# Hybrid attention layer on one core: float32 products of the head tasks moved behind the rounded ones, and some head steps moved later

## The chip, the cores and the metric

The kernel runs on one core of a Trainium2 chip. A core has TensorE (PE, matrix products; its weight loads are listed apart as PEld), VectorE (DVE), ScalarE (ACT), GpSimd (POOL) and SyncE (SP, which only issues transfers). The metric is the device time of one execution in microseconds; three runs of the kernel before took 1094.37, 1094.30 and 1093.46 us, so its median is 1094.3 us.

## What is computed

One layer of a streaming encoder, 256 tokens of width 2048, all float32, cut here to what matters:

```python
h  = rms_norm(x, attn_norm)
qa, ka, va, fa, qb, kb, vb = split(h @ w_in)          # 8 + 8 heads of width 128
# forgetting heads: q and k normed per head, c = cumsum(log_sigmoid(fa + b))
logits = q @ k.T * scale + c[t] - c[s]                # causal
out_a  = softmax(logits) @ va
# stick-breaking heads
z = qb @ kb.T * scale                                 # strictly causal
suffix = reverse_cumsum(log_sigmoid(z) - z) - itself
out_b  = exp(log_sigmoid(z) + suffix) @ vb
x = x + concat(rms_norm(out_a), rms_norm(out_b)) @ w_out
x = x + conv_ffn(rms_norm(x))                         # up, conv of 3, SiLU gate, down
```

## The kernel before

Every weight matrix is streamed in pieces of 1 MB and multiplied in three rounded products: a piece is split into a high part (w_hi, a cast on ScalarE, L263) and a low part (w_lo, a subtraction on VectorE, L271), the tokens likewise, and high x high, high x low and low x high are summed in PSUM. A *step* is one such piece. In the stage of the heads a step's products are twelve of 512 columns (L291; eight with w_hi, four with w_lo), or twice that. The order on every engine is the order in which the Python code issues the instructions. In each round of the main loop, the weights of the step two ahead are split, those six ahead are loaded, the step's products are issued, and then `tick()` is called; steps of 24 products call it a second time in their middle.

`tick()` is what weaves the heads between the weight products. Each head is a Python generator; `running` holds those under way, and a tick advances each of them to its next `yield`. A new head starts at the earliest three ticks after the last. So a head's instructions of one `yield` stretch stand on each engine between the products of two steps, and the next stretch follows one tick later.

A forgetting head (`fox_head`) goes through these stretches. First it splits its queries and keys into rounded parts (qk, L725 and L726). Two ticks later come the scores in PSUM tile ps_s: a rounded product of 384 columns with the forget sums (L731), the first 128 x 128 block in full float32 (L734, which TensorE runs as two passes), and three rounded products of 256 columns for the second block (L736); then VectorE adds the mask and takes the maxima (L739 to L742). Two ticks later ScalarE takes exponentials and VectorE normalises (L748 to L753). Two ticks later TensorE transposes the three blocks of weights into ps_p (L758, float32). One tick later they are split (pT, L763 to L765). One tick later, two where the head's number divides by four, they are multiplied with the values into ps_o: three rounded products (`weighted`, L709) and a float32 one (L710). One tick later the output is scaled and squared for the norm.

A stick-breaking head (`sb_head`) multiplies its queries and keys in float32 right at its start (ps_z, L785 and L786), and masks them on VectorE (L789). One tick later ScalarE runs three activations and VectorE one operation (e, L792 to L795). Two ticks later that is split (sps, L799 and L800). Two ticks later the running sums are added in ps_z by rounded products: for the high part one of 384 columns (L805) and one of 128 (L806), then the same for the low part. One tick later come the exponential and its split (w and ws, L809 to L813), one tick later `weighted` (the last head has float32 products only, L821), and one tick later the output.

Other float32 products of the stage are the transposes of queries and keys when a group of four heads is ready (ps_h, L637) and a few small sums (pg, L927). Head tiles in PSUM share four banks. At the end of the stage the heads still running are advanced inside the output projection, whose last products need their results.

Of the kernel before, what the change touches and what calls it, by code (L numbers as in the profile page):

```python
# [15 lines left out]
P = 128  # L16
D = 2048
S = 256
# [3 lines left out]
NH = 8  # L22
# [16 lines left out]
LOAD, SUM, SPLIT = 6, 4, 2  # L39
WARM = 4, 2  # L40
STAGGER = 3
FFN_PARTS = [(f, min(f + 8, NFT)) for f in range(0, NFT, 8)]


@with_exitstack
def hybrid_layer(
# [19 lines left out]
    nc = tc.nc  # L66
# [153 lines left out]
    steps, following, after, waiting, running, others = [], [], [], deque(), [], []  # L220
# [8 lines left out]
    def advance(tasks):  # L229
        tasks[:] = [g for g in tasks if next(g, g) is not g]  # L230

    def tick():
        ticks[0] += 1
        if waiting and ticks[0] - ticks[1] >= STAGGER:
            running.append(waiting.popleft())
            ticks[1] = ticks[0]
        advance(running)
        advance(others)

    def acc_tile(name):  # L240
# [88 lines left out]
    ntri = masksR[:, 2 * P :]  # L329
# [341 lines left out]
    def sb_rows(half):  # L671
        def done(rows):
            while started["fox"] < NH or started["sb"] < 4 * half:
                yield
            if half:
                yield
                yield
            yield from to_heads(rows, (f"qB{half}", f"kB{half}"), (QSCALE, 1.0))
            ready.add(f"qB{half}")
            if "vB" in ready:  # L680
                start_sb(half)

        return done
# [22 lines left out]
    def weighted(po, hi, lo, v1, w, w1):  # L706
        mm = nc.tensor.matmul
        for m, (v, i) in enumerate(((hi, 0), (hi, 1), (lo, 0))):
            mm(po, v, w[:, i, :S], start=m == 0, stop=False)  # L709
        mm(po[:, P:], v1, w1, start=False, stop=True)  # L710

    def squared(po, group, h):
# [7 lines left out]
    def fox_head(h, half):  # L720
        q, k = tile_of[f"qA{half}"][:, h % 4, :], tile_of[f"kA{half}"][:, h % 4, :]
        hi, lo, v1 = tile_of["vA"]
        qk = tmp.tile([P, 2, 3 * P], F32R, name="qk", tag="sps")
        for c, whole in ((slice(0, P), q[:, P:]), (slice(P, 3 * P), k)):
            act.copy(qk[:, 0, c], whole)  # L725
            dve.tensor_tensor(qk[:, 1, c], whole, f32(qk[:, 0, c]), op=ALU.subtract)  # L726
        yield
        yield
        ps = psb.tile([P, 512], F32, name="ps_s", tag="t")[:, : 3 * P].rearrange("p (a b) -> p a b", a=3)
        s0, s1 = ps[:, 0, :], ps[:, 1:3, :].rearrange("p a b -> p (a b)")  # L730
        nc.tensor.matmul(  # L731
            ps.rearrange("p a b -> p (a b)"), headR[:, h : h + 1].to_broadcast([P, P]), cR, start=True, stop=False
        )
        nc.tensor.matmul(s0, q[:, :P], k[:, :P], start=False, stop=False)  # L734
        for a, b in ((0, 0), (0, 1), (1, 0)):
            nc.tensor.matmul(s1, qk[:, a, :P], qk[:, b, P:], start=False, stop=a == 1)  # L736
        started["fox"] += 1
        diagonal = ps[:, 0::2, :]
        dve.tensor_tensor(diagonal, diagonal, maskF, op=ALU.add)  # L739
        nm = small.tile([P, NT], F32, name="nm", tag="nm", bufs=4)  # L740
        dve.tensor_reduce(nm[:, 0:1], s0, axis=AX.X, op=ALU.max, negate=True)
        dve.tensor_reduce(nm[:, 1:2], s1, axis=AX.X, op=ALU.max, negate=True)  # L742
        yield
        yield
        l = small.tile([P, NT], F32, name="l", tag="l", bufs=4)
        pr = tmp.tile([P, 3, P], F32, name="pr", tag="pr")
        p0, p1 = pr[:, 0, :], pr[:, 1:3, :].rearrange("p a b -> p (a b)")
        act.activation(p0, s0, AF.Exp, bias=nm[:, 0:1], accum_out=l[:, 0:1])  # L748
        act.activation(p1, s1, AF.Exp, bias=nm[:, 1:2], accum_out=l[:, 1:2])
        rl = small.tile([P, NT], F32, name="rl", tag="rl", bufs=4)  # L750
        dve.reciprocal(rl, l)
        dve.tensor_scalar(p0, p0, rl[:, 0:1], None, op0=ALU.mult)
        dve.tensor_scalar(p1, p1, rl[:, 1:2], None, op0=ALU.mult)  # L753
        yield
        yield
        pt = psb.tile([P, 512], F32, name="ps_p", tag="t")[:, : 3 * P].rearrange("p (a b) -> p a b", a=3)
        for i in range(3):
            nc.tensor.transpose(pt[:, i, :], pr[:, i, :], ident)  # L758
        yield
        pT = tmp.tile([P, 2, 3 * P], F32R, name="pT", tag="sps")  # L760
        p1 = tmp.tile([P, 3 * P], F32, name="p1", tag="pT")[:, :P]
        flat = pt.rearrange("p a b -> p (a b)")
        act.copy(pT[:, 0, :S], flat[:, :S])  # L763
        act.copy(p1, flat[:, S:])
        dve.tensor_tensor(pT[:, 1, :S], flat[:, :S], f32(pT[:, 0, :S]), op=ALU.subtract)  # L765
        yield
        if h % 4 == 0:
            yield
        po = psb.tile([P, S], F32, name="ps_o", tag="t")
        hs = slice(h * HD, (h + 1) * HD)  # L770
        weighted(po, hi[:, hs], lo[:, hs], v1[:, hs], pT, p1)
        yield
        act.activation(oFox[:, h, :], po, AF.Identity, scale=g_fox[:, h : h + 1])
        sq = squared(po, 0, h)
        if sq is not None:
            dve.tensor_tensor(ssq[0], ssq[0], sq, op=ALU.add)

    def sb_head(h, half):
        q, k = tile_of[f"qB{half}"][:, h % 4, :], tile_of[f"kB{half}"][:, h % 4, :]
        (hi, lo), v1 = tile_of["vB01"], tile_of["vB"][half, 1]  # L780
        ps = psb.tile([P, 512], F32, name="ps_z", tag="t")[:, : 3 * P].rearrange("p (a b) -> p a b", a=3)
        z0, z1 = ps[:, 0:2, :].rearrange("p a b -> p (a b)"), ps[:, 2, :]
        zz = ps.rearrange("p a b -> p (a b)")
        mm = nc.tensor.matmul
# [9 lines left out]
        act.activation(e, e, AF.Ln, bias=1.0)  # L794
        dve.scalar_tensor_tensor(e, zz, 0.0, e, op0=ALU.max, op1=ALU.add)  # L795
        yield
        yield
        sps = tmp.tile([P, 2, 3 * P], F32R, name="sps", tag="sps")
        act.copy(sps[:, 0, :], e)  # L799
        dve.tensor_tensor(sps[:, 1, :], e, f32(sps[:, 0, :]), op=ALU.subtract)  # L800
        yield
        yield
        for i in range(2):
            s = sps[:, i, :]
            mm(zz, ntri[:, :P], s, start=False, stop=False, skip_group_check=True)  # L805
            mm(ps[:, 1, :], ntri[:, P:], s[:, 2 * P :], start=False, stop=i == 1, skip_group_check=True)  # L806
        yield
        w = tmp.tile([P, 3 * P], F32, name="w", tag="pT")
        act.activation(w, zz, AF.Exp)  # L809
        if h < NH - 1:  # L810
            ws = tmp.tile([P, 2, 3 * P], F32R, name="ws", tag="sps")
# [3 lines left out]
        po = psb.tile([P, S], F32, name="ps_o", tag="t")  # L815
        hs = slice((h % 4) * HD, (h % 4 + 1) * HD)
        h0 = slice(h * HD, (h + 1) * HD)
        if h < NH - 1:
            weighted(po, hi[:, h0], lo[:, h0], v1[:, hs], ws, w[:, S:])
        else:  # L820
            mm(po, tile_of["vB"][half, 0][:, hs], w[:, :S], start=True, stop=False)  # L821
            mm(po[:, P:], v1[:, hs], w[:, S:], start=False, stop=True)
        yield
# [465 lines left out]
    for f_lo, f_hi in FFN_PARTS:  # L1289
# [5 lines left out]
        if last is None:  # L1295
            behind = []
# [5 lines left out]
        behind = deque(behind)  # L1302
# [116 lines left out]
```

## Time and profile before

| what | value |
|---|---|
| runs of the kernel before, median | 1094.3 us |
| profiled execution, span from the first to the last instruction | 1091.8 us |
| TensorE busy in it | 1087.3 us, 5701 products |
| VectorE busy | 924.2 us |
| ScalarE busy | 755.1 us |
| read from memory | 255.48 MB, 236 GB/s over the span |

The profile is of one execution. It gives no total of its own for that execution beside the span; the median lies 2.5 us above the span, which is what is outside the first and last instruction. In timelines a row gives the start and the length in us from the span's start, the engine, the line of the kernel, what is written from what, the shape and how many alike follow each other. Matmuls are pipelined, so that the records overlap: what a product takes from its engine is read from one start to the next, not from its length. A number in square brackets is idle time ahead of a row and who ended it. A list of waits gives the sum, the times and the longest. A row of windows gives, for each engine, busy time and instructions, then the granted clock of TensorE, the share of the DMA engines and GB/s.

### The profile page before, as it was taken

The page shows a single profiled execution, that of the slowest core. Times are in us where ns is not written, and L with a number is a line of the kernel's source. Part 1 is how long each engine was busy: PE and PEld are TensorE (multiplying, and loading weights), DVE is VectorE, ACT ScalarE, POOL GpSimd, SP SyncE. Part 2 cuts the span into 40 slices and gives each one's busy share as a digit, 9 for nine tenths or more (in the row PEclk, how much of TensorE's full clock was granted, in tenths as well). Part 3 has the DMA queues.
Part 4 walks back from the last instruction along what each step waited for, and adds up shares of the span by engine and source line. Part 5 has one row for each costly group of instructions (what it writes and reads, how often), then busy time and mean ns, then how long its engine had stood idle before and what let it go on. Part 6 is the DMA issues. An engine that isn't in the chain of part 4 may idle for free.

```text
span 1091.8 us, 14685 instructions
## 1 busy us (share of the span) xinstructions
PE 1087.3 (100%) x5701; PEld 939.5 (86%) x5701; DVE 924.2 (85%) x918; ACT 755.1 (69%) x968; POOL 59.0 (5%) x53
## 2 busy tenths in 40 slices
PE   9999999999999999999999999999999999999998
PEld 9988888888888888888888888888888888888887
DVE  5988899888897667779887988889898889879996
ACT  6767697767766657767766776677667767667763
POOL 0000000001000000000000000100000000000000
PEclk9999999999999999999999999999999999999999
DMA  8897886868777465669989597996969799896995
GB/s 310 276 272 239 271 206 196 253 183 271 239 214 251 154 199 161 214 170 249 288 206 316 173 265 254 254 296 170 302 195 271 241 246 279 215 319 161 291 247 155
DMA packets 175215, 258.53 MB, mean 237 GB/s; under 512 B 4632, under 2 KB 98218, under 8 KB 175146
## 3 DMA queue, kind: packets, MB, share of 16 engines
q1 hardware_dynamic: 151690, 210.26, 56.9%
q0 software_dynamic: 23280, 47.19, 24.5%
q8 instruction: 45, 0.74, 0.3%
q14 instruction: 24, 0.20, 0.1%
q10 hardware_dynamic: 176, 0.14, 0.0%
HBM read 255.48 MB, written 2.10 MB: 236 GB/s over the span
## 4 chain that ended last, share of the span: by engine, by line
PE 100%; DVE 0%; issue 0%
PE pu L1153 45%; PE bank_a L291 18%; PE bank_b L291 11%; PE bank_c L291 6%; PE acc_o L291 6%; PE acc_v L411 4%; PE bank_e L291 2%; PE acc L291 2%; PE ps_x L192 1%; PE ps_h L637 1%; PE ps_o L709 1%; PE ps_z L785 0%; PE ps_o L710 0%; PE ps_z L805 0%; PE ps_i L186 0%; PE half L291 0%
## 5 line engine op out<-in xcount | busy, mean ns | idle before, releaser
L271 DVE TENSOR_TENSOR w_lo<-w_raw,w_hi 128x2048 fp32r<-128x2048 f32 (+2 forms) x251 | 555.9, 2219 | 124.1 <-ACT w_hi L263 123.1
L263 ACT CAST w_hi<-w_raw 128x2048 fp32r<-128x2048 f32 (+2 forms) x251 | 464.6, 1854 | 220.7 <-PE pu L1153 90.0
L1153 PE MATMUL pu<-hT,w_hi 128*128 128x512 f32 x1408 | 333.6, 390 | 0.0
L1153 PEld LDWEIGHTS pu<-hT,w_hi 128*128 128x128 f32 x1408 | 263.1, 188 | 53.6
L1153 PEld LDWEIGHTS pu<-hT,w_lo 128*128 128x128 f32 x1408 | 180.0, 191 | 6.5
L1153 PE MATMUL pu<-hT,w_lo 128*128 128x256 f32 x1408 | 182.1, 283 | 0.0
L1206 POOL DMA_DIRECT2D w_raw<-in_w_down_dram x31 | 39.8, 1302 | 715.9 <-DVE w_lo L271 384.7
L1078 ACT ACTIVATE tap<-up,ccol 128x256 f32<-128x256 f32 x176 | 74.6, 495 | 0.0
L291 PE MATMUL bank_a<-w_hi,hT 128*128 128x512 f32 x192 | 48.5, 395 | 0.0
L291 PEld LDWEIGHTS bank_a<-w_hi,hT 128*128 128x128 f32 x192 | 35.2, 188 | 6.7
L291 PE MATMUL bank_b<-w_hi,s 128*128 128x512 f32 x160 | 40.1, 393 | 0.0
L291 PE MATMUL bank_a<-w_hi,s 128*128 128x512 f32 x160 | 40.0, 392 | 0.0
L291 PE MATMUL bank_a<-w_hi,g 128*128 128x512 f32 x152 | 38.0, 392 | 0.0
L411 PE MATMUL acc_v<-w_hi,hT 128*128 128x344 f32 x192 | 35.7, 328 | 0.0
L291 PEld LDWEIGHTS bank_b<-w_hi,s 128*128 128x128 f32 x160 | 28.8, 189 | 5.5 <-issue 0.3
L291 PEld LDWEIGHTS bank_a<-w_hi,s 128*128 128x128 f32 x160 | 28.9, 189 | 5.2
L1083 DVE TENSOR_TENSOR gate<-gate,tap 128x512 f32<-128x512 f32 x44 | 30.3, 689 | 2.7 <-DVE gate L1083 0.5
L1083 DVE TENSOR_TENSOR val<-val,tap 128x512 f32<-128x512 f32 x44 | 30.3, 689 | 2.3
L291 PE MATMUL acc_o<-w_hi,oSb 128*128 128x512 f32 x128 | 31.8, 397 | 0.0
L1064 DVE TENSOR_TENSOR up<-t,R 128x512 f32<-128x512 f32 x44 | 30.5, 692 | 1.5
L291 PEld LDWEIGHTS bank_a<-w_hi,g 128*128 128x128 f32 x152 | 27.4, 189 | 4.9
L411 PEld LDWEIGHTS acc_v<-w_hi,hT 128*128 128x128 f32 x192 | 30.4, 190 | 0.5 <-DVE hT L203 0.2
(293 smaller groups left out, 1411.2 us busy)
## 6 DMA issues: line engine op xcount, KB each, us to landing
w_raw<-in_w_up_dram SPq DMA_DIRECT2D x88, 1024.0 KB, 7.0
w_raw<-in_w_down_dram SPq DMA_DIRECT2D x44, 1024.0 KB, 6.7
w_raw<-in_w_in_dram SPq DMA_DIRECT2D x40, 1024.0 KB, 5.5
w_raw<-in_w_down_dram POOLq DMA_DIRECT2D x31, 1024.0 KB, 9.8
w_raw<-in_w_out_dram SPq DMA_DIRECT2D x16, 1024.0 KB, 7.7
w_raw<-in_w_in_dram POOLq DMA_DIRECT2D x10, 1024.0 KB, 9.4
w_raw<-in_w_in_dram SPq DMA_DIRECT2D x13, 516.0 KB, 5.5
xb<-in_x_dram POOLq DMA_DIRECT2D x4, 512.0 KB, 8.7
```

Of the source, the lines that this page charges most:

```text
L192: nc.tensor.transpose(ps[:, j, t * P : (t + 1) * P], x2[:, t, (k + j) * P : (k + j + 1) * P], ident)
L263: copy(hi[:, :n], raw[:, :n])
L271: dve.tensor_tensor(lo[:, :n], raw[:, :n], f32(hi[:, :n]), op=ALU.subtract)
L291: nc.tensor.matmul(o, lhs(i, l, t), r[:, i, :] if cut is None else r[:, i, cut], start=starts and j == 0, stop=stops and j == 3 * n - 1, s ...
L411: nc.tensor.matmul(banks[j][t][:, :VC], of_half(hT[:, k], l, t), w[:, 0, m * VC : (m + 1) * VC], start=k == l == 0 and w is mem["parts", i ...
L637: nc.tensor.transpose(ps[:, h, :], rows[n, t][:, h * HD : (h + 1) * HD], ident)
L709: mm(po, v, w[:, i, :S], start=m == 0, stop=False)
L1064: dve.tensor_tensor(u[:, :, 2:], t2, R, op=ALU.mult)
L1078: act.activation(taps[w][:, j, :], u[:, j, w : w + S], AF.Copy, scale=ccol[:, w, f : f + 1])
L1083: dve.tensor_tensor(a, a, tap, op=ALU.add)
L1153: nc.tensor.matmul(acc[:, j, S:] if low else acc[:, j, :], (lo if low else hi)[:, i, j * P : (j + 1) * P], hT[:, k, 0, :] if low else hT[: ...
L1206: nc.gpsimd.dma_start(mem[weights].rearrange("p (a b) -> p a b", a=4), plus, accum_op=ALU.add)
```

## The change

The order in which a tick advances the heads is made of two passes. A head may now stop with `yield FLOATS`. In the first pass every head is advanced by one `yield`; those that stopped with `FLOATS` are then advanced once more, in a second pass of the same tick. So the rounded products of all heads in a tick stand ahead of their float32 ones. `FLOATS` stands ahead of the float32 scores, the transposes, the float32 product of `weighted` and the first scores of stick-breaking.

Some steps also move in time. In forgetting heads 0 to 6 the transposes come four ticks after the exponentials instead of two, and the weighting two ticks after the split of the transposed weights, instead of one (two for heads 0 and 4). Head 7 keeps its distances. A stick-breaking head makes its first scores one tick after its start instead of at once; its split (sps) follows the activations after one tick instead of two, so that the later parts keep their distance from the start of the head. The queries and keys of the second group of stick-breaking heads are transposed one tick earlier. The sums are ordered as two products of 384 columns and then two of 128. The number and the shapes of the instructions are the same.

```diff
+    def advance_heads():
+        kept, behind = [], []
+        for g in running:
+            said = next(g, g)
+            if said is not g:
+                kept.append(g)
+            if said == FLOATS:
+                behind.append(g)
+        advance(behind)
+        running[:] = kept
...
-        advance(running)
+        advance_heads()
         advance(others)
...
             if half:
                 yield
-                yield
             yield from to_heads(rows, (f"qB{half}", f"kB{half}"), (QSCALE, 1.0))
...
             mm(po, v, w[:, i, :S], start=m == 0, stop=False)
+        yield FLOATS
         mm(po[:, P:], v1, w1, start=False, stop=True)
...
-        nc.tensor.matmul(s0, q[:, :P], k[:, :P], start=False, stop=False)
         for a, b in ((0, 0), (0, 1), (1, 0)):
-            nc.tensor.matmul(s1, qk[:, a, :P], qk[:, b, P:], start=False, stop=a == 1)
+            nc.tensor.matmul(s1, qk[:, a, :P], qk[:, b, P:], start=False, stop=False)
+        yield FLOATS
+        nc.tensor.matmul(s0, q[:, :P], k[:, :P], start=False, stop=True)
...
-        yield
-        yield
+        aligned = h < NH - 1
+        for _ in range(4 if aligned else 2):
+            yield
+        yield FLOATS
         pt = psb.tile([P, 512], F32, name="ps_p", tag="t")[:, : 3 * P].rearrange("p (a b) -> p a b", a=3)
...
-        if h % 4 == 0:
+        if aligned:
             yield
...
         (hi, lo), v1 = tile_of["vB01"], tile_of["vB"][half, 1]
+        yield
+        yield FLOATS
         ps = psb.tile([P, 512], F32, name="ps_z", tag="t")[:, : 3 * P].rearrange("p (a b) -> p a b", a=3)
...
         dve.scalar_tensor_tensor(e, zz, 0.0, e, op0=ALU.max, op1=ALU.add)
         yield
-        yield
         sps = tmp.tile([P, 2, 3 * P], F32R, name="sps", tag="sps")
...
         for i in range(2):
-            s = sps[:, i, :]
-            mm(zz, ntri[:, :P], s, start=False, stop=False, skip_group_check=True)
-            mm(ps[:, 1, :], ntri[:, P:], s[:, 2 * P :], start=False, stop=i == 1, skip_group_check=True)
+            mm(zz, ntri[:, :P], sps[:, i, :], start=False, stop=False, skip_group_check=True)
+        for i in range(2):
+            mm(ps[:, 1, :], ntri[:, P:], sps[:, i, 2 * P :], start=False, stop=i == 1, skip_group_check=True)
```

What stands in a row on TensorE around the fourth forgetting head's scores, before (ps_o is a weighting, p and pT its float32 and rounded operands, ps_s scores, ps_p transposes of weights, ps_h transposes of queries and keys, bank_ weight products):

```order
L709 MATMUL ps_o<-pT,vA_712 128x256 x2
L709 MATMUL ps_o<-pT,vA_713 128x256
L710 MATMUL ps_o<-p_1554,vA_714 128x128
L731 MATMUL ps_s<-cR,headR 128x384
L734 MATMUL ps_s<-kA_1190,qA_1222 128x128
L736 MATMUL ps_s<-qk 128x256 x3
L291 MATMUL bank_b<-w_hi,hT 128x512 x8
L291 MATMUL bank_b<-w_lo,hT 128x512 x4
L758 MATMUL ps_p<-cs,pr 128x128 x3
L637 MATMUL ps_h<-cs,rB_1045 128x128 x4
L637 MATMUL ps_h<-cs,rB_1046 128x128 x4
```

The same place after the change:

```order
L720 MATMUL ps_o<-pT,vA_712 128x256 x2
L720 MATMUL ps_o<-pT,vA_713 128x256
L743 MATMUL ps_s<-cR,headR 128x384
L747 MATMUL ps_s<-qk 128x256 x3
L722 MATMUL ps_o<-p_1515,vA_714 128x128
L773 MATMUL ps_p<-cs,pr 128x128 x3
L749 MATMUL ps_s<-kA_1190,qA_1222 128x128
L303 MATMUL bank_b<-w_hi,hT 128x512 x8
L303 MATMUL bank_b<-w_lo,hT 128x512 x4
L649 MATMUL ps_h<-cs,rB_1045 128x128 x4
L649 MATMUL ps_h<-cs,rB_1046 128x128 x4
```

Three float32 runs (L710, L734, and L758 with L637) have become two: the float32 products of weighting, transposes and scores stand in one run behind all rounded ones. The weighting is now that of the first head, where it was that of the second.

TensorE around the third stick-breaking head's first scores (ps_z; the weighting is that of the first head), before:

```order
L785 MATMUL ps_z<-qB_2093,kB_2060 128x256
L786 MATMUL ps_z<-qB_2093,kB_2060 128x128
L291 MATMUL bank_b<-w_hi,sums 128x512 x8
L291 MATMUL bank_b<-w_lo,sums 128x512 x4
L709 MATMUL ps_o<-ws,vB_2285 128x256 x2
L709 MATMUL ps_o<-ws,vB_2286 128x256
L710 MATMUL ps_o<-w,vB_1874 128x128
L291 MATMUL bank_c<-w_hi,hT 128x512 x8
```

And after:

```order
L303 MATMUL bank_b<-w_hi,sums 128x512 x8
L303 MATMUL bank_b<-w_lo,sums 128x512 x4
L720 MATMUL ps_o<-ws,vB_2285 128x256 x2
L720 MATMUL ps_o<-ws,vB_2286 128x256
L722 MATMUL ps_o<-w,vB_1870 128x128
L802 MATMUL ps_z<-qB_2080,kB_2046 128x256
L803 MATMUL ps_z<-qB_2080,kB_2046 128x128
L303 MATMUL bank_c<-w_hi,hT 128x512 x8
```

The first scores stand one step later, behind the float32 product of the weighting, so two runs have become one.

VectorE around the fifth and sixth stick-breaking heads (ws: the low parts that the fifth head's weighting needs; xb: rows of the output projection; sps: the split of the sixth head), before:

```order
L795 SCALAR_TENSOR_TENSOR e<-ps_z,e 128x384
L900 SCALAR_TENSOR_TENSOR xb<-bank_a,nrg_127,xb 128x512
L271 TENSOR_TENSOR w_lo<-w_raw,w_hi 128x2048
L900 SCALAR_TENSOR_TENSOR xb<-bank_b,rg_125,xb 128x512
L271 TENSOR_TENSOR w_lo<-w_raw,w_hi 128x2048
L813 TENSOR_TENSOR ws<-w,ws 128x256
L800 TENSOR_TENSOR sps<-e,sps 128x384
L789 TENSOR_TENSOR ps_z<-ps_z,masksR 128x2x128
```

And after:

```order
L812 SCALAR_TENSOR_TENSOR e<-ps_z,e 128x384
L917 SCALAR_TENSOR_TENSOR xb<-bank_a,nrg_127,xb 128x512
L283 TENSOR_TENSOR w_lo<-w_raw,w_hi 128x2048
L829 TENSOR_TENSOR ws<-w,ws 128x256
L816 TENSOR_TENSOR sps<-e,sps 128x384
L917 SCALAR_TENSOR_TENSOR xb<-bank_b,rg_125,xb 128x512
L283 TENSOR_TENSOR w_lo<-w_raw,w_hi 128x2048
L806 TENSOR_TENSOR ps_z<-ps_z,masksR 128x2x128
```

ws and sps stand ahead of one row update and one subtraction of weights, where they stood behind them. On TensorE the fifth head's weighting has moved ahead by half a step as well, from the middle of the next step's products to the end of the step before.

More of the change, by code (lines that the diff above doesn't have):

```diff
@@ L41 @@
 STAGGER = 3
+FLOATS = "float32 products"
 FFN_PARTS = [(f, min(f + 8, NFT)) for f in range(0, NFT, 8)]
@@ L770, in fox_head @@
         hs = slice(h * HD, (h + 1) * HD)
-        weighted(po, hi[:, hs], lo[:, hs], v1[:, hs], pT, p1)
+        yield from weighted(po, hi[:, hs], lo[:, hs], v1[:, hs], pT, p1)
         yield
@@ L818, in sb_head @@
         if h < NH - 1:
-            weighted(po, hi[:, h0], lo[:, h0], v1[:, hs], ws, w[:, S:])
+            yield from weighted(po, hi[:, h0], lo[:, h0], v1[:, hs], ws, w[:, S:])
         else:
+            yield FLOATS
             mm(po, tile_of["vB"][half, 0][:, hs], w[:, :S], start=True, stop=False)
```

## The prediction

> **What bounds the kernel now.** I read the page first, then the stage of the heads alone (busy time by windows), then who waits on TensorE, then TensorE's timeline product by product. The page:
>
> ```profile
> span 1091.8 us, 14685 instructions
> PE 1087.3 (100%) x5701; PEld 939.5 (86%) x5701; DVE 924.2 (85%) x918; ACT 755.1 (69%) x968; POOL 59.0 (5%) x53
> PEclk9999999999999999999999999999999999999999
> PE 100%; DVE 0%; issue 0%
> ```
>
> The chain that ended last is TensorE and nothing else, at a granted clock in the top tenth from end to end. The profiled execution's span is 1091.8 us; the median of the runs is 1094.3, so 2.5 us lie around the span, and I leave them as they are. The heads (forgetting from 133 us, stick-breaking to 350 us) are the only stretch that the change touches. Busy time in it, and all that TensorE's weight loads wait for from 150 us on:
>
> ```profile
> 133.00:350.00 217.00, 217.00 (x1070) 183.29 (x1069) 194.03 (x226) 161.11 (x255) 13.16 (x12) 1.00 0.76 224
> ```
>
> ```profile
> PEld ps_o L709 <- DVE ws L813: 0.2, 1, 0.2
> PEld ps_h L637 <- ACT kB L641: 0.2, 1, 0.2
> PEld ps_o L821 <- ACT w L809: 0.2, 1, 0.2
> ```
>
> TensorE is busy for all 217 us of the stage. Three waits of 0.2 us are the whole list. VectorE works 194 of the 217 us, so it has 11% to spare. The time is therefore the sum of TensorE's own steps, from one product's start to the next, and what the change can win is what it does to those steps. A busy share doesn't show them, because the records of products overlap; their starts do. TensorE's timeline around the second head's scores and the first head's transposes (start, length, what, how many):
>
> ```profile
> 142.44 0.34 PE L731 MATMUL ps_s<-cR,headR 128*128 128x384 f32 x1
> 142.62 0.38 PE L734 MATMUL ps_s<-kA,qA 128*128 128x128 f32 x2
> ...
> 143.19 2.02 PE L291 MATMUL bank_c<-w_hi,hT 128*128 128x512 f32 x8
> ...
> 145.97 0.49 PE L758 MATMUL ps_p<-cs,pr 128*128 128x128 f32 x3
> 146.21 2.10 PE L291 MATMUL bank_b<-w_hi,sums 128*128 128x512 f32 x8
> ...
> 149.05 1.98 PE L291 MATMUL bank_e<-w_hi,hT 128*128 128x512 f32 x8
> 150.87 1.07 PE L291 MATMUL bank_e<-w_lo,hT 128*128 128x512 f32 x4
> 151.77 0.34 PE L731 MATMUL ps_s<-cR,headR 128*128 128x384 f32 x1
> ```
>
> A step of twelve 512-column products with nothing before it takes 151.77 - 149.05 = 2.72 us, its first eight 1.82. After a float32 product, the next rounded product's start stands too early by some 0.08 us and its length is as much longer (eight in 146.21 to 149.05 less four: the step has 2.84). So I always count from the first product of a float32 run to the end of the twelve products behind it. Two more such places, a forgetting head's weighting and a stick-breaking head's first scores:
>
> ```profile
> 173.43 0.52 PE L709 MATMUL ps_o<-pT,vA 128*128 128x256 f32 x3
> 173.78 0.38 PE L710 MATMUL ps_o<-p,vA 128*128 128x128 f32 x2
> 173.92 2.07 PE L291 MATMUL bank_c<-w_hi,hT 128*128 128x512 f32 x8
> ...
> 176.74 0.49 PE L758 MATMUL ps_p<-cs,pr 128*128 128x128 f32 x3
> ```
>
> ```profile
> 246.17 0.59 PE L785 MATMUL ps_z<-qB,kB 128*128 128x256 f32 x2
> 246.60 0.38 PE L786 MATMUL ps_z<-qB,kB 128*128 128x128 f32 x2
> 246.74 2.08 PE L291 MATMUL bank_e<-w_hi,hT 128*128 128x512 f32 x8
> ...
> 249.56 0.39 PE L291 MATMUL bank_b<-w_hi,hT 128*128 128x512 f32 x1
> ```
>
> A float32 product stands as two passes. One of 256 columns takes (246.60 - 246.17) / 2 = 0.215, so one of 128 columns 0.1075; a transpose is one such pass. A rounded product of 256 columns takes (173.78 - 173.43) / 3 = 0.117, one of 384 columns 142.62 - 142.44 = 0.18.
>
> **Part 1: fewer changes between the two kinds.** What a float32 run costs beyond its own products:
> - scores, float32 in the middle: 145.97 - 142.44 = 3.53; bare 0.18 + 2 x 0.1075 + 3 x 0.117 + 2.72 = 3.47; extra 0.06.
> - transposes alone: 149.05 - 145.97 = 3.08; bare 3 x 0.1075 + 2.72 = 3.04; extra 0.04.
> - weighting: 176.74 - 173.43 = 3.31; bare 0.35 + 0.215 + 2.72 = 3.285; extra 0.025.
> - first scores of stick-breaking: 249.56 - 246.17 = 3.39; bare 0.43 + 0.215 + 2.72 = 3.365; extra 0.025.
>
> The products are the same before and after; only their order differs. Counted in TensorE's order from the end of the opening to the first up-projection, there are 49 unbroken float32 runs before and 37 after: 12 fewer. The mean of the four extras is 0.0375, so 12 x 0.0375 = 0.45 us. Bounds: 12 x 0.025 = 0.3 and 12 x 0.06 = 0.72. Nothing hides this, and nothing takes it back elsewhere, since TensorE is the path.
>
> [...] The rows show 0.025 to 0.06 at each run, so I keep them.
>
> **Part 2: the second sums of stick-breaking** (two of 384 columns, then two of 128, where they alternated). Their rows:
>
> ```profile
> 261.12 0.34 PE L805 MATMUL ps_z<-sps,masksR 128*128 128x384 f32 x1
> 261.30 0.22 PE L806 MATMUL ps_z<-sps,masksR 128*128 128x128 f32 x1
> 261.36 0.39 PE L805 MATMUL ps_z<-sps,masksR 128*128 128x384 f32 x1
> 261.59 0.22 PE L806 MATMUL ps_z<-sps,masksR 128*128 128x128 f32 x1
> 261.65 2.05 PE L291 MATMUL bank_a<-w_hi,sums 128*128 128x512 f32 x8
> 263.54 1.07 PE L291 MATMUL bank_a<-w_lo,sums 128*128 128x512 f32 x4
> ```
>
> To the end of the next eight it is 2.42 us; less 2 x 0.18 and 1.82, the two narrow ones cost 0.12 each, though their own starts are 0.06 apart from the next: what follows a narrow product begins late. In the new order two products still follow a narrow one, so I take 0. Bounds: if the second narrow one came for 0.06, 8 x 0.06 = 0.5 us are won; a loss of as much if both narrow ones delayed the next product twice.
>
> **Part 3: moved steps and waits.** Transposes come two calls later, the weighting two or three, the stick-breaking first scores one later, their second sums not. Nothing is added on any queue; SP's and POOL's orders don't change, so no transfer moves in order. On ScalarE and VectorE the copies and subtractions of weights keep their places; two or three short operations (0.4 us each) pass them. In a forgetting head's scores the float32 part now comes last, behind other heads' float32 products, so VectorE's mask can start two to five passes later (0.2 to 0.6 us). What hides that is the subtraction of weights that stands ahead of the mask on VectorE (2.29 us, row below); without it VectorE's spare time would. Of the three waits, the first is at the fifth stick-breaking head's weighting:
>
> ```profile
> 320.34 2.29 DVE L271 TENSOR_TENSOR w_lo<-w_raw,w_hi 128x2048 fp32r<-128x2048 f32 x1 [0.16 <-ACT w_hi L263]
> 322.55 0.74 DVE L900 SCALAR_TENSOR_TENSOR xb<-bank_b,rg,xb 128x512 f32<-128x512 f32 x1
> ...
> 326.46 0.42 DVE L813 TENSOR_TENSOR ws<-w,ws 128x256 fp32r<-128x256 f32 x1
> ```
>
> ```profile
> 323.36 0.59 PE L785 MATMUL ps_z<-qB,kB 128*128 128x256 f32 x2
> ...
> 326.76 0.68 PE L709 MATMUL ps_o<-ws,vB 128*128 128x256 f32 x3
> 327.28 0.38 PE L710 MATMUL ps_o<-w,vB 128*128 128x128 f32 x2
> ```
>
> Here three products take 0.52 where they take 0.35 above: 0.17 lost, because the low parts end at 326.88. In the new order VectorE makes them right behind the subtraction that starts at 320.34, so by 323.0, and TensorE asks at about 323.5: the wait goes, with 0.5 us in hand. The second wait (transposes of the last queries) loses its neighbour and goes too; the third stays. That is 0 to 0.4 won. Steps that move can as well run into new waits of that size; the trace can't show them. I take 0.15 won, bounds 0.4 won and 0.5 lost.
>
> Sum: 0.45 + 0 + 0.15 = 0.6 us. Span 1091.8 - 0.6 = 1091.2; time 1094.3 - 0.6 = **1093.7 us**. About 0.2% (2.2 us) is what a measurement of this kernel can tell from no change, so I forecast no change that can be told.
>
> **Rivals.**
> - *The changes of kind cost nothing* (what I read there is how starts are recorded): only the waits remain, 1094.3 - 0.15 = 1094.15. For it: 0.025 is little above the rows' rounding. Against: four kinds of place all come out positive. Chance 0.15. [...]
> - *Everything at its upper bound*: 0.72 + 0.5 + 0.4 = 1.6, 1092.7. Chance 0.08.
> - *Slower: ScalarE stands behind the softplus.* In stick-breaking heads the split of the sums (sps) now follows the exponential chain after one call instead of two. ScalarE takes things in order; if VectorE's part of the chain waits behind one subtraction of weights (2.29 us, row above), ScalarE's next cast waits too. It does such a thing already:
>
> ```profile
> 251.39 0.49 ACT L792 ACTIVATE e<-ps_z 128x384 f32<-128x384 f32 x1 [1.91 <-DVE ps_z L789]
> 318.41 1.89 ACT L263 CAST w_hi<-w_raw 128x2048 fp32r<-128x2048 f32 x1
> 323.93 2.99 PE L291 MATMUL acc_o<-w_hi,hT 128*128 128x512 f32 x12
> ```
>
> The cast that ends at 320.30 is first used at 323.93, 3.6 us ahead. It decides when two heads in a row lose 2.29 without making it up: 2 x 2.29 - 3.6 = 1.0 us, 1095.3 less what the runs win; three, 3.3 us, 1097. Against: VectorE's spare 11% and ScalarE's 26% (161 of 217) make up 2.29 us within a few steps. Chance 0.1 for about 1 us, 0.03 for over 2.2.
> - *The clock falls.* The longest float32 run grows to 15 passes (two of a weighting, three transposes, two of scores, eight transposes), 15 x 0.1075 = 1.6 us. If TensorE's clock halved over such a run it would take 1.6 us more, 1095.3. Every row of the stage has 1.00, runs of eight and eleven transposes among them. Chance 0.01. [...]
>
> That the change doesn't do what it says is excluded by the order of its instructions, which has the runs as counted.
>
> **Numbers.** The forecast itself (0.3 to 1.2 us won) has 0.63. The range runs from 1092.7 to 1095.0: below, the upper bounds of the parts; above, no gain and the scatter of the runs shown or a wait of half a us. Faster by over 0.2% would take more than 2.2 us, over all bounds together: 0.03, which is for scatter. Slower by over 0.2%: 0.04, from the third rival's far end. Within: 0.93.
>
> **What would show it.** Step 1 right: in the new trace a score step (rounded scores, float32 part, twelve products) takes 3.50 to 3.51 instead of 3.53, and where weighting, scores and transposes share a run the whole costs about 0.04 over its bare products. Part 2: 2.42 us again. Part 3: the weighting at 323.5 takes 0.35, and the first two waits are gone from the list. Wrong: a span below 1090, or new waits of over 0.5 us on TensorE, or twelve plain products off 2.72.

## The result and the profile after

| | before | after |
|---|---|---|
| median of five runs | 1093.58 us | 1099.58 us |
| lowest to highest | 1093.32 to 1094.37 | 1099.30 to 1100.34 |
| span of the profiled execution | 1091.8 us | 1097.8 us |

The ratio is 1.0051, with a 95% interval from 1.0040 to 1.0062: the change costs 6 us, far outside the forecast range (1092.7 to 1095.0) and on the side that had 0.04. Both medians lie 1.8 us above the spans, so the whole difference lies inside the span. The page of the kernel after (span, busy time, granted clock, chain):

```profile
span 1097.8 us, 14669 instructions
PE 1089.5 (99%) x5701; PEld 941.5 (86%) x5701; DVE 924.9 (84%) x918; ACT 755.5 (69%) x968; POOL 59.0 (5%) x53
PEclk9999999999999999999999999999999999999999
PE 96%; DVE 2%; ACT 2%; issue 1%; DVEq 0%; ACTq 0%
```

The work is the same: every engine has the same number of instructions as before (the total of the page, which counts more than these, is smaller by 16). VectorE and ScalarE are busy for 0.7 and 0.4 us more, TensorE for 2.2 (its slower products are seen below). The chain of before was TensorE alone; now 4% of it lie on VectorE and ScalarE. So TensorE has begun to wait, and the list of waits says for whom. A new wait of over 0.5 us on TensorE was among the prediction's signs of being wrong. After (engine, line, releaser; sum, times, longest), and below it the one row that changed most on ScalarE, in the kernel before:

```profile
PE ps_o L720 <- DVE ws L829: 1.8, 1, 1.8
PE bank_a L303 <- ACT rD L618: 1.4, 1, 1.4
PE ps_h L649 <- DVE rs_a L169: 0.6, 1, 0.6
ACT e L809 <- DVE ps_z L806: 10.2, 6, 4.1
ACT sps L815 <- DVE e L812: 5.5, 4, 2.0
```

```profile
ACT e L792 <- DVE ps_z L789: 6.5, 6, 1.9
```

Before, none of the three TensorE waits existed. They sit in the stick-breaking heads, within some 30 us. TensorE's timeline there (start, length, what, how many; in brackets the idle time ahead):

```profile
267.59 0.28 PE L720 MATMUL ps_o<-ws,vB 128*128 128x256 f32 x1
269.65 0.51 PE L720 MATMUL ps_o<-ws,vB 128*128 128x256 f32 x2 [1.78 <-DVE ws L829]
269.99 0.58 PE L722 MATMUL ps_o<-w,vB 128*128 128x128 f32 x2
...
271.51 2.98 PE L303 MATMUL bank_c<-w_hi,hT 128*128 128x512 f32 x8
274.33 1.08 PE L303 MATMUL bank_c<-w_lo,hT 128*128 128x512 f32 x4
...
281.65 0.38 PE L722 MATMUL ps_o<-w,vB 128*128 128x128 f32 x2
...
282.44 2.08 PE L303 MATMUL bank_a<-w_hi,hT 128*128 128x512 f32 x8
284.37 1.07 PE L303 MATMUL bank_a<-w_lo,hT 128*128 128x512 f32 x4
...
287.69 1.07 PE L303 MATMUL bank_c<-w_lo,hT 128*128 128x512 f32 x4
290.19 2.12 PE L303 MATMUL bank_a<-w_hi,hT 128*128 128x512 f32 x8 [1.43 <-ACT rD L618]
...
297.36 0.62 PE L649 MATMUL ps_h<-cs,rD 128*128 128x128 f32 x4
298.58 0.65 PE L649 MATMUL ps_h<-cs,rD 128*128 128x128 f32 x4 [0.59 <-DVE rs_a L169]
```

Counted from start to start, the stalls cost 269.65 - 267.59 - 0.12 = 1.94 us, 290.19 - 287.69 - 0.91 = 1.59 (four 512-column products take 0.91), and 298.58 - 297.36 - 0.43 = 0.79: 4.3 us together. The rest stands right behind the first stall. From the weighting's float32 product to the end of the next eight weight products it takes 274.33 - 269.99 = 4.34 us; the same instructions a little later take 284.37 - 281.65 = 2.72. Those 1.6 us are the clock, which the 40 slices of the page are too coarse to show. The same execution by windows (the number after the POOL column is the granted clock):

```profile
267.50:270.50 3.00, 1.22 (x8) 0.90 (x7) 3.00 (x5) 3.00 (x3) 2.45 (x4) 0.92 0.32 64
270.50:274.00 3.50, 3.50 (x12) 2.85 (x11) 3.50 (x4) 1.92 (x5) 0.42 (x1) 0.58 0.88 307
```

At half clock (0.50 from 270.04 to 273.46), a mean of 0.58 over 3.50 us is 2.94 us of it, and 0.92 over 3.00 us 0.48: together 3.42 us at half speed, which would cost half of it, 1.7. With the 1.6 read from the starts, 4.3 + 1.6 = 5.9 us, which is the difference of the spans (6.0) to 0.1.

**Where the first stall comes from.** ScalarE and VectorE of the kernel after, ahead of it:

```profile
262.87 0.49 ACT L809 ACTIVATE e<-ps_z 128x384 f32<-128x384 f32 x1 [2.70 <-DVE ps_z L806]
...
264.38 1.90 ACT L275 CAST w_hi<-w_raw 128x2048 fp32r<-128x2048 f32 x1
```

```profile
257.41 2.29 DVE L283 TENSOR_TENSOR w_lo<-w_raw,w_hi 128x2048 fp32r<-128x2048 f32 x1 [1.25 <-ACT w_hi L275]
...
260.20 2.29 DVE L283 TENSOR_TENSOR w_lo<-w_raw,w_hi 128x2048 fp32r<-128x2048 f32 x1
262.41 0.42 DVE L806 TENSOR_TENSOR ps_z<-ps_z,masksR 128x256 f32<-128x256 f32 x1
...
266.31 2.29 DVE L283 TENSOR_TENSOR w_lo<-w_raw,w_hi 128x2048 fp32r<-128x2048 f32 x1 [1.24 <-ACT w_hi L275]
...
269.18 0.41 DVE L829 TENSOR_TENSOR ws<-w,ws 128x256 fp32r<-128x256 f32 x1
```

And before, the same activations, cast, subtractions, mask and ws:

```profile
257.97 0.49 ACT L792 ACTIVATE e<-ps_z 128x384 f32<-128x384 f32 x1 [0.28 <-DVE ps_z L789]
...
260.42 1.91 ACT L263 CAST w_hi<-w_raw 128x2048 fp32r<-128x2048 f32 x1 [0.84 <-PE bank_b L291]
```

```profile
254.83 2.29 DVE L271 TENSOR_TENSOR w_lo<-w_raw,w_hi 128x2048 fp32r<-128x2048 f32 x1 [0.81 <-ACT w_hi L263]
...
257.51 0.43 DVE L789 TENSOR_TENSOR ps_z<-ps_z,masksR 128x256 f32<-128x256 f32 x1
...
262.36 2.29 DVE L271 TENSOR_TENSOR w_lo<-w_raw,w_hi 128x2048 fp32r<-128x2048 f32 x1 [1.76 <-ACT w_hi L263]
...
265.23 0.42 DVE L813 TENSOR_TENSOR ws<-w,ws 128x256 fp32r<-128x256 f32 x1
```

Read it as a loop; these rows are its second turn, at the second head. The first turn, at the first head's mask, has already made VectorE's subtraction start at 257.41 instead of 254.83. The first scores come a tick later, so the mask stands behind one more subtraction of weights on VectorE (2.29 us, at 260.20): with the first turn's delay it is done at 262.8, not 257.9. ScalarE's rows keep the order of the code: it stands idle for 2.70 us ahead of the activations (262.87), and its next cast, issued behind them, starts at 264.38 instead of 260.42. VectorE's next subtraction needs that cast. VectorE was idle for it before as well (1.76); now it is idle first for the activations (1.67, until 264.51; not among these rows) and then for the cast (1.24), and the subtraction starts at 266.31 instead of 262.36. ws, the low parts of the first head's weighting, stands behind that: 269.18 instead of 265.23. TensorE asked at 267.6. The two engines wait for one another in turns, and each turn holds up the other's queue. I call this the convoy below.

**Where the second stall comes from.** It is the wait on rD, and it hangs on sps, not on a mask:

```profile
288.45 0.55 DVE L812 SCALAR_TENSOR_TENSOR e<-ps_z,e 128x384 f32<-128x384 f32 x1
289.04 0.51 ACT L815 CAST sps<-e 128x384 fp32r<-128x384 f32 x1 [1.74 <-DVE e L812]
```

sps now follows the activations after one tick. ScalarE stands idle at it for VectorE's e, which stands behind a subtraction and other work; rD comes next on ScalarE (289.46), and TensorE starts again at 290.19. Of the kernels below, this wait stands in each that has both the later first scores and the closer sps, and in no other. The third wait, on rs_a, comes with the second group's transposes, which G below moves.

### The profile page after: what moved, and what is told of

Read it like the earlier page. It is cut to its first block, busy times and chain, and to the rows that moved or that the text cites. A ratio compares the mean times of both kernels' runs of the same rounds, so it can differ in the third digit from the quotient of the medians.

```text
span 1097.8 us, 14669 instructions
## 1 busy us (share of the span) xinstructions
PE 1089.5 (99%) x5701; PEld 941.5 (86%) x5701; DVE 924.9 (84%) x918; ACT 755.5 (69%) x968; POOL 59.0 (5%) x53
## 4 chain that ended last, share of the span: by engine, by line
PE 96%; DVE 2%; ACT 2%; issue 1%; DVEq 0%; ACTq 0%
PE pu L1170 44%; PE bank_a L303 17%; PE bank_b L303 10%; PE bank_c L303 6%; PE acc_o L303 6%; PE acc_v L423 4%; PE acc L303 2%; PE bank_e L303 2%; ACT w_hi L275 1%; DVE w_lo L283 1%; PE ps_x L193 1%; PE ps_h L649 1%; PE ps_o L720 0%; PE ps_o L722 0%; PE ps_i L187 0%
```

## The experiments

Two shifts of stick-breaking work are in the change: **S**, first scores one tick later and sps one tick closer to the activations; **G**, the second group's transposes, and with them heads 4 to 7, one tick earlier. The third column adds ScalarE's two waits for VectorE in this chain (activations on the mask, sps on e): 6.5 + 2.0 us before, 10.2 + 5.5 after. A batch of kernels ran on one chip with the kernel before, whose median was 1093.99, 1094.03, 1093.88 and 1093.95 us in the four batches.

| kernel | median us (ratio, 95%) | ScalarE waits for VectorE | TensorE waits in the stage, us |
|---|---|---|---|
| after less S | 1098.31 (1.0025 to 1.0054) | 16.5 | 1.6, 0.8, 1.7 |
| before with S | 1099.68 (1.0037 to 1.0070) | 21.6 | 1.8, 2.7, 0.3 |
| after, sps two ticks behind | 1099.61 (1.0037 to 1.0067) | 16.4 | 1.3, 2.8 |
| after, first scores at once | 1098.60 (1.0027 to 1.0057) | 16.0 | four on ws, 3.1 in all |
| after less S and G | 1093.96 (0.9990 to 1.0009) | 8.4 | none |
| before with G | 1099.08 (1.0032 to 1.0062) | 16.6 | 1.6, 0.8, 1.7 |
| grouping alone | 1094.09 (0.9993 to 1.0012) | 8.5 | none |
| before with later forgetting heads | 1093.69 (0.9987 to 1.0006) | 8.3 | none |
| after, mask on TensorE | 1097.00 (1.0016 to 1.0035) | 3.4 | 1.3, 0.6 |
| before with G, mask on TensorE | 1096.24 (1.0013 to 1.0032) | none | 1.6 |
| before, mask on TensorE | 1095.74 (1.0005 to 1.0023) | 1.6 | 0.7 |
| before, first scores later | 1099.54 (1.0031 to 1.0061) | 18.6 | 1.3, 2.8 |
| before, sps closer | 1096.24 (1.0012 to 1.0030) | 10.8 | 0.6, 1.4 |
| after less G | 1099.78 (1.0032 to 1.0066) | 19.4 | 1.8, 1.4, 0.3 |

### First batch: the two halves of S

After less S:

```diff
-        yield
         yield FLOATS
         ps = psb.tile([P, 512], F32, name="ps_z", tag="t")...
...
         yield
+        yield
         sps = tmp.tile([P, 2, 3 * P], F32R, name="sps", tag="sps")
```

> The changed kernel, with the stick-breaking heads' times of before: first scores in the first tick (still behind the rounded products of that tick), the split sps two ticks after the activations. Theory A (a later first score puts the mask behind one more subtraction of weights on VectorE; ScalarE stands idle for it with its casts queued behind, and the products of weighting wait in the end): the waits of TensorE of 1.8 us on ws and 1.4 us on rD are gone, and the granted clock is 1.00 throughout; about 1093.1 us (0.5 below before, as the lag stood at 240 us), or 1094 if the wait of the transposes on rs_a stays. Rival B (the grouping or the later forgetting heads disturb the stage, the stick-breaking times do not matter): 1098 us or more.

Measured: 1098.31 us, no slow clock (1.00 in each window from 133.00 to 353.00, where the kernel after has 0.74 from 267.50 to 274.00). The waits on ws and rD at the first group are gone, as theory A had it, but three others stand at heads 4 to 7. By the time alone rival B had won; the next batch shows that what was left is G.

Before with S alone (one `yield` ahead of ps_z, one less ahead of sps):

> The kernel before, with only the stick-breaking heads' first scores one tick later and sps one tick after the activations: no grouping, no moved forgetting steps, sums as before. Theory A: 1097 us or more, with a wait of over 1 us for ws at the first stick-breaking head's weighting. Rival B: 1093.6 us within 0.5.

Measured: 1099.68, with 1.8 us on ws at the first head: theory A, and B's 1093.6 is out. S alone costs 5.7 us.

After, with the second `yield` ahead of sps put back:

> The changed kernel, but sps again two ticks after the activations, so that a stick-breaking head as a whole is one tick later. Theory A: ScalarE still stands idle some 4 and 2.7 us for the masks of the first two heads, but weighting comes a tick (2.7 us) later, which covers the 1.8 us; sps no longer stands right behind the chain: 1093 to 1095 us. Rival B: 1098 us or more.

Measured: 1099.61. Theory A's forecast missed. A tick more for the weighting doesn't cover the wait; it stays on ws, at 1.3 and 2.8 us.

After, with the `yield` ahead of `yield FLOATS` in sb_head taken out:

> The changed kernel, but first scores in a stick-breaking head's first tick, while sps stays one tick after the activations (so all later parts come one tick earlier). Theory A: the mask has its old place, so the idle time of ScalarE ahead of the activations falls to about that of before (1.9, 0.3, 0.8 us), but w and ws are asked for a tick earlier, and sps stands right behind the chain: between 1093 and 1099 us; above 1096 if the distance from activations to sps is what costs, below 1095 if the later mask is. Rival B: 1098 us or more.

Measured: 1098.60, four waits on ws of up to 1.5 us. This kernel holds G too, so that it decides nothing about S; the idle time at the masks was 14.3 us, not the old one.

### Second batch: everything but the shifts, and G alone

After less S and G (both edits above, and `yield` twice again in sb_rows):

> The changed kernel with everything that moves stick-breaking work in time undone: first scores in the first tick, sps two ticks after the activations, the second group's transposes at their old tick. What is left is the grouping, the later forgetting heads and the order of the sums. Theory A (every shift of stick-breaking work against the weight steps costs a wait of 1 to 3 us in a stretch where ScalarE and VectorE have no slack; grouping and forgetting heads win a little): 1093.4 us or less, no wait of TensorE over 0.5 us in the stage of the heads. Rival B (the grouping or the later forgetting heads disturb the stick-breaking stage themselves): 1096 us or more.

Measured: 1093.96, ratio 1.0000, no wait of TensorE in the stage. Theory A's gain (1093.4 or less) did not come, but rival B falls: grouping, later forgetting heads and the order of the sums cost nothing, and win nothing that can be told.

Before with one line less:

```diff
             if half:
                 yield
-                yield
             yield from to_heads(rows, (f"qB{half}", f"kB{half}"), (QSCALE, 1.0))
```

> The kernel before with one line less: the second group of stick-breaking queries and keys is transposed one tick earlier, and with it heads 4 to 7 start a tick earlier. Theory A: a wait of 1 to 2 us for rs_a at the transposes, and one or two more at heads 4 to 7, as in the kernel with the stick-breaking times undone (1.6, 0.8 and 1.7 us there): 1096 to 1098 us. Rival (this line only costs in company of the others): 1094 us.

Measured: 1099.08, 5 us for one `yield`, more than expected. Its waits (the one on rs_a I read as the shared bank of pg, which VectorE's rs_a sets free; the other two of TensorE as the convoy at heads 4 to 7):

```profile
PE bank_a L291 <- ACT sps L798: 1.7, 1, 1.7
PE ps_h L637 <- DVE rs_a L168: 1.6, 1, 1.6
PE acc_o L291 <- DVE xb L988: 0.8, 1, 0.8
ACT e L791 <- DVE ps_z L788: 16.6, 7, 6.0
```

ScalarE stands idle for masks for 16.6 us in place of 6.5, as with S, though here nothing was made later. The rows of the fifth head show how: in the kernel before, a weight cast (306.04) stands ahead of its activations on ScalarE. A tick earlier they stand ahead of such a cast, the mask is still behind VectorE's other work (done at 308.73), and ScalarE is idle for 5.07 us with two casts queued behind, which start at 310.27.

Grouping and the order of the sums alone (after, with every `yield` of before):

> The changed kernel with every step at its tick of before: only the grouping of float32 products behind the rounded ones and the order of the sums. By the changes of kind at 0.0375 us each: 0.3 to 0.5 us below before. If changes of kind cost nothing: equal to before. If the second pass itself brings waits: above before.

Measured: 1094.09, equal to before, so the gain of 0.3 to 0.5 us did not show. (This kernel has only four float32 runs fewer than before, 0.15 us at 0.0375 each.)

Before with the forgetting heads' later steps alone (four ticks to the transposes, two to the weighting):

> The kernel before with only the forgetting heads' transposes two ticks later and the weighting two ticks after the split: no grouping. No wait appeared in this stretch of the changed kernel, so equal to before within 0.3 us; if the last forgetting heads push later work, the wait shows at the start of the stick-breaking stage (240 to 260 us).

Measured: 1093.69, equal to before, and no new wait.

### Third batch: the mask taken out of VectorE's queue

```diff
-        dve.tensor_tensor(diagonal, diagonal, maskB, op=ALU.add)
+        mm(diagonal, identR, masksR[:, P : 2 * P].unsqueeze(1).to_broadcast([P, 2, P]), start=False, stop=True, skip_group_check=True)
```

> The changed kernel, with the causal mask of the stick-breaking scores added in PSUM by one rounded product of 256 columns with the identity on TensorE, instead of by VectorE. ScalarE's activations then wait for TensorE alone. The products cost 8 x 0.12 = 1.0 us. Theory C (convoy: the mask stands behind subtractions of weights on VectorE, ScalarE stands idle for it with its next casts queued behind, and the next subtraction waits for those): ScalarE's idle time ahead of the activations falls from 10.2 us to under 3, the 1.8 us wait on ws and the clock drop behind it go, 1096 us or less. Rival D (ScalarE and VectorE simply have no time left in this stretch for steps that come later, whatever waits for what): 1099 us or more.

Measured: 1097.00. ScalarE waits for TensorE now, 1.9 us in all, and the cast that started at 264.38 in the kernel after starts as early as before:

```profile
260.53 1.91 ACT L275 CAST w_hi<-w_raw 128x2048 fp32r<-128x2048 f32 x1 [0.24 <-PE bank_b L303]
```

The wait on ws and the slow clock are gone (the run's mean clock is 1.000, after 0.998). That is 2.6 us less than the kernel after in spite of what the products cost. The 1096 of theory C was missed by 1.0: the other two waits (1.3 on rD, which hangs on sps, and 0.6 on rs_a) don't hang on this mask. By the time alone, rival D's 1099 is out. The edit also takes eight masks of 0.42 us from VectorE, though, so that this run doesn't keep the waiting apart from the work. The windows ahead of the first stall do, in the kernel after and then before:

```profile
255.00:267.50 12.50, 12.50 (x59) 10.48 (x58) 7.70 (x7) 9.67 (x14) 0.00 (x0) 1.00 1.07 323
255.00:267.50 12.50, 12.50 (x60) 10.53 (x59) 10.74 (x11) 10.24 (x13) 0.00 (x0) 1.00 1.08 330
```

VectorE is busy for 7.70 of the 12.50 us right ahead of the stall, where it was for 10.74, and ScalarE for 9.67 where it was for 10.24. Both had time left there; VectorE's idle times end with ScalarE's activations and casts, ScalarE's with VectorE's mask.

> The kernel before with the second group a tick earlier (1099.1 us) and the mask on TensorE as in the run above. Theory C: the wait of the transposes on rs_a (1.6 us) stays, since it has nothing to do with the mask; the waits of 0.8 on xb and 1.7 on ScalarE's cast go: 1099.1 + 1.0 - 2.5 - up to 1 of slow starts behind them, so 1096.5 to 1097.6. Rival D: 1100 us.

Measured: 1096.24, 2.8 us less than with G alone. The wait on rs_a stays at 1.6, the other two are gone. That is theory C's mechanism on a kernel in which S plays no part, 0.3 us below its range.

> The kernel before with the mask on TensorE: the price of the products by themselves. No wait of TensorE hangs on the mask there, so about 1094.0 + 1.0 = 1095.0 us by both theories; less only if the mask delays something that the trace does not show.

Measured: 1095.74: 1.9 us, not 1.0. A step with the mask's product takes 259.30 - 255.77 = 3.53 us where it took 3.39, so eight take 1.1; 0.7 is a new wait on ws. So the edit is no improvement, and taking its price off, the convoy was worth more than the 2.6 to 2.8 us that came back.

The fourth kernel measures TensorE's clock and repeats casts of weights, so that it takes longer (1128.96 us, one execution); what is computed is that of before.

```diff
         copy(hi[:, :n], raw[:, :n])
+        extra = stalled.pop() if stalled else 0
+        while extra > 0:
+            m = min(extra, n)
+            copy(hi[:, :m], raw[:, :m])
+            extra -= m
...
+        if n >= FFN + 10 and (n - FFN) % 14 == 10:
+            stalled[:] = [2048 * 3 + 512 * ((n - FFN) // 14 % 9)]
```

> The kernel before, with one weight cast in every fourteenth step of the feed-forward stage repeated for 5.5 to 9 us more, so that TensorE stands idle for some 0 to 5 us, once every 40 us or so (what is computed stays the same). [...]

Three of its stalls, and the windows behind the first two:

```profile
521.34 1.88 PE L1160 MATMUL pu<-hT,w_hi 128*128 128x512 f32 x7 [1.80 <-ACT w_hi L269]
...
766.93 5.30 PE L1160 MATMUL pu<-hT,w_hi 128*128 128x512 f32 x15 [1.86 <-ACT w_hi L269]
...
649.18 2.06 PE L298 MATMUL bank_b<-w_hi,s 128*128 128x512 f32 x8 [2.16 <-DVE xb L1182]
```

```profile
521.47:524.88 3.41, 3.41 (x16) 2.80 (x17) 3.41 (x2) 3.41 (x3) 0.00 (x0) 1.00 0.04 5
767.24:770.65 3.41, 3.41 (x9) 2.65 (x8) 3.38 (x2) 3.41 (x4) 0.00 (x0) 0.50 0.30 59
```

1.80 us idle leaves the clock at 1.00, 1.86 is followed by 3.41 us at 0.50, and 1.00 again from 770.65. Behind the longer one of 2.16 us the clock stays at 1.00 (647.77 to 651.18, and on to 654.60). A stall of 3.29 us that ends at 957.09 is followed by 0.50 from 958.40 to 961.79. Behind one of 2.83 us twelve products of 256 columns take 2.93 us (at 1037.30), where sixteen take 2.07 at 644.95 and a clock of 1.00; I read that as half clock too. So the length of a stall alone doesn't say what follows it, and what else does isn't shown. No stall of this run is longer than 3.3 us.

### Fourth batch: S taken apart on the kernel before

First scores later, the rest of the head with them:

```diff
         (hi, lo), v1 = tile_of["vB01"], tile_of["vB"][half, 1]
+        yield
         ps = psb.tile([P, 512], F32, name="ps_z", tag="t")...
```

> The kernel before with only the later first scores: every later part of a stick-breaking head one tick later too. The convoy theory: ScalarE's idle time ahead of the activations rises from 6.5 to over 10 us, and TensorE waits somewhere for work that the held-up casts or splits delay: 1096 us or more. If only the closer distance from activations to sps costs: 1094 us.

Measured: 1099.54, the convoy's side. Its rows (the longer wait on ws is followed by half clock, 0.50 from 295.90 to 299.20):

```profile
ACT e L793 <- DVE ps_z L790: 18.6, 7, 4.1
PE ps_o L709 <- DVE ws L814: 4.2, 2, 2.8
```

sps closer alone (one `yield` less ahead of sps):

> The kernel before with only one line less: sps one tick after the activations, first scores at their old tick, so sums, weighting and output come a tick earlier. The convoy theory: the masks keep their places, ScalarE's idle time ahead of the activations stays near 6.5 us for the first heads; what comes a tick earlier (ws for weighting) is waited for only where it had under 2.7 us in hand: 1094 to 1096 us. If the closer distance is what costs: 1097 us or more.

Measured: 1096.24, a little above the convoy's 1094 to 1096 and under the 1097 of the other reading. The masks keep their places (5.2 us), and ScalarE's idle time moves to sps:

```profile
ACT sps L798 <- DVE e L795: 5.6, 5, 2.8
```

After less G:

> The changed kernel with the second group's transposes at their old tick. The wait of 0.6 us on rs_a goes; the two waits of the first group (1.8 and 1.4 us) and the clock drop stay: 1098.5 us, or 1 us less if the late first scores of heads 4 to 7 then meet their masks earlier, 1 us more if later.

Measured: 1099.78, 1.3 us above the 1098.5. The wait on rs_a is gone, but the time is that of the kernel after: where S stands, G costs nothing more. Neither stall of the first group needs G: 1.8 and 1.4 us are the same here.

## Why the prediction was wrong, point by point

- **What bounds the kernel: right.** TensorE's steps were the sum of the time, and what the change did shows as TensorE's starts.
- **Part 1, fewer changes of kind: right in kind, too large.** A score step was to take 3.50 to 3.51, and steps in which weighting, transposes and scores share a run 0.04 over their products:

```profile
143.05 0.34 PE L743 MATMUL ps_s<-cR,headR 128*128 128x384 f32 x1
...
146.55 1.98 PE L303 MATMUL bank_b<-w_hi,sums 128*128 128x512 f32 x8
...
161.27 0.52 PE L720 MATMUL ps_o<-pT,vA 128*128 128x256 f32 x3
...
165.67 1.03 PE L649 MATMUL ps_h<-cs,rB 128*128 128x128 f32 x8
```

  The first (146.55 - 143.05) is 3.50. The second (165.67 - 161.27) is 4.40 us for 4.35 of products (0.35 + 0.18 + 0.35 + 0.215 + 0.32 + 0.215 + 2.72): 0.05. But the term was counted as runs times a mean. In after less S and G, which has nine runs fewer, all in the forgetting heads, these heads take 0.19 us less than before (a product that stood 0.54 behind at their start, at 140.26 against 139.72, stands 0.35 behind at their end, 243.79 against 243.44): 0.02 each, so 0.25 for the twelve where I had 0.45. Grouping alone has four runs fewer and no gain that can be told. The first rival had 0 here; the runs lie between that and my term.
- **Part 2, the order of the sums: right.** After less S and G takes 3.32 us for a step with them (264.79 - 261.47), before 3.33 (264.45 - 261.12). In the kernel after, such a sum takes 2.42 us to the end of the next eight (285.27 to 287.69), as forecast.
- **Part 3, moved steps and waits: here it failed.** The fifth head's weighting and the last transposes (those of the queries) no longer wait, as said, nor does the last head's weighting, which was to go on waiting for 0.2. The failed step is "I take 0.15 won, bounds 0.4 won and 0.5 lost" with "the trace can't show them". The waits and the slow clock behind one of them cost 5.9 of the 6.0 us, and the trace could have shown where to look. For every instruction that moved past a weight subtraction I asked how long it was, not what stands behind it on its engine. The mask is 0.4 us long; ScalarE's next cast hangs on it through the activations, and VectorE's next subtraction on that. G has no term in the prediction at all: the list of moved steps there leaves out the second group's transposes and with them the earlier heads 4 to 7. G alone cost 5.0 us.
- **The third rival had the mechanism, with the wrong slack and too small a chance.** It saw ScalarE held up in this chain, but priced it by the cast's own use on TensorE, 3.6 us ahead, "when two heads in a row lose 2.29 without making it up". The cast's first user is VectorE, though, not TensorE: the prediction's own row for the subtraction at 320.34 has 0.16 us of idle time that this very cast ended, at 320.30. The slack there was nothing, where 3.6 us were counted. The path that closed first is cast, subtraction, ws, weighting: ws was done at 265.65 in the kernel before and asked for at 267.85, so 2.2 us in hand; it came 4 us later. The case that this rival spelled out, ScalarE held up at sps, is the second stall of 1.4 us. And it was let off by the averages, "VectorE's spare 11% and ScalarE's 26%". Both engines had that idle time after the change as well; it lay where one waited for the other.
- **The clock rival was right on what it looked at, and looked at the wrong thing.** The longer float32 runs left the clock alone (1.00 in the forgetting heads). A stall of 1.78 us did not (0.50 behind it). I had no price for a wait beyond its own length; here one wait of 1.8 us cost 3.5.
- **What stays open.** S and G are not additive (5.7 and 5.0 us alone, 6.0 with all the rest), nor are the halves of S (5.6 us for the first scores, with the rest of the head a tick later, and 2.3 for sps alone). A stall of TensorE hands the other engines the time that they had lost, so that a later wait has less to lose; that is argued, not shown. That the second group's transposes wait because pg holds one of the four shared banks is read from the releaser, and wasn't tried. Of the kernels none beats before: the parts that are not S or G win 0.1 to 0.3 us at most, which these runs can't tell from nothing.

## What to carry to other kernels

When a change moves a short instruction past a long one on an engine whose rows keep the order of the code (here the 0.42 us mask behind the 2.29 us subtraction), follow what hangs on it through the other engine's queue and back, and compare the delay with the least slack on that loop, not with the slack of the instruction itself. Spare busy time of two engines that feed each other was no cover (VectorE was busy for 7.70 and ScalarE for 9.67 of the 12.50 us ahead of the stall): look at who ends their idle times, since here 8.5 us of ScalarE's waiting for VectorE went with 1094 us, and over 15 us with 1098 and above, as long as the mask stayed on VectorE. A step of a schedule that is already woven is best moved alone first: one `yield` was worth 5 us.

## What the runs showed of the hardware

Some stalls of TensorE were followed by half clock, and others of about the same length were not:

| run | stall, us | granted clock behind it |
|---|---|---|
| after | 1.78 | 0.50 (270.04 to 273.46), then 1.00 |
| before with S | 1.8 | 1.00 (267.50 to 274.00, and on to 287.00) |
| before with repeated casts | 1.80 | 1.00 (521.47 to 524.88) |
| before with repeated casts | 1.86 | 0.50 (767.24 to 770.65), then 1.00 |
| before with repeated casts | 2.16 | 1.00 (647.77 to 654.60) |
| before with S | 2.68 | 1.00 (287.00 to 299.00) |
| before, first scores later | 2.8 | 0.50 (295.90 to 299.20), then 1.00 |
| before with repeated casts | 3.29 | 0.50 (958.40 to 961.79) |

The cost comes on top of the stall: in the kernel after, the slow stretch of 3.42 us cost 1.6 us beyond the stall itself. The shortest stall with half clock behind it is 1.78 us and the longest without is 2.68, so in these runs no length divides the two; what does isn't shown.
